# Order of the first loads and block norms, key products by feature tile, output slabs ahead of x, and pooled means in place

## The chip, the cores and the metric

The kernel runs on one core of a Trainium2 chip. The metric is the device time of the whole program in microseconds (us). The engines are TensorE (PE, with its weight loads listed apart as PEld), VectorE (DVE), ScalarE (ACT), GpSimd (POOL) and SyncE (SP), whose queue issues all DMA transfers of this kernel. Each engine runs its own instructions in the order that was fixed when the program was built. Semaphores make it wait for other engines.

## The reference

Two layers of a backbone run on 1024 latent tokens and 128 context tokens with 1024 features. Cut to what matters:

```python
shift1, scale1, gate1, shift2, scale2, gate2 = split(silu(cond) @ w_mod[l] + b_mod[l])
x = x + gate1 * mixer_l(rms_norm(x, g) * (1 + scale1) + shift1)
x = x + gate2 * conv_ffn(rms_norm(x, g2) * (1 + scale2) + shift2)
# layer 0: z = h @ w_in; queries, compressed keys/values and gated MLP from z; mixer = [attention | gMLP] @ w_out
c_kv = rms_norm(kv_c, g_kv)                   # 256 columns of z, beside 32 rotary ones
# layer 1: z = h @ w_in; mixer = [conv(a * sigmoid(gate)) | pool(p)] @ w_out
win = cs[:, hi, g] - cs[:, lo, g]             # window sums of 2, 4, 8, 16 tokens for four groups of 128 channels
pool = win / cnt - p                          # cnt is smaller at both ends of a sequence
pool = einsum("blgc,gcd->blgd", pool, w_pool) * s_pool
```

Outputs are both token sets after two layers, the normalised compressed keys/values and their rotary part for the context. Products are kept close to float32 by splitting each operand into a high and a low part and adding three products.

## The kernel before

**Tiling.** Features lie on the 128 partitions, in 8 feature tiles (`KT`). Tokens lie along the free side: 1154 columns, in three blocks `BLK` of 384, 384 and 386 (the last one holds 256 latent tokens, 2 empty columns and 128 context tokens). A normalised block is `hb[b]`, with a high and a low part for each feature tile. `mm3` (L74) issues the three products of one feature tile. `unit` (L54) loads a slab of weights into a `raw` buffer and splits it with ACT (L66) and DVE (L67) into a `wt` buffer; `weights(r, w)` says how many of each there are. PSUM has six banks `gp` for products and two `sm` for small ones.

**Order.** The program is written as one stream of calls. A planner with a model of the times gives each engine its fixed order: an instruction that is ready in the model goes first by its place in the stream, and `later(offset)` moves that place back. `fill` is a list of small steps, above all the modulation steps, which `drip` puts into the stream a few at a time with such an offset. `issue_after(ins)` keeps the instructions in its block behind `ins` on the same engine. `follow(a, b)` makes `a` wait for `b`.

**The start** (`even`, L463). Block 0 of x is loaded whole (L478). `mod_pe` (L118) loads eight slabs of w_mod for one chunk of the modulation (L124) and multiplies them on PE (L126). It runs for the scale (chunk 1) and then for the shift (chunk 0). `norm_blk` (L295) norms a block: ACT squares each feature tile (L257), the squares are added (`sq_sums`, L243: on DVE at L261 in the blocks of `FASTB`, else in pairs on POOL and DVE, L270 to L273), PE sums over partitions (L281), POOL takes the root (L589), PE spreads it (L290), DVE scales each feature tile in x itself (L318), and ACT and DVE write the shifted high and low parts into `hb` (L87, L88). For blocks 1 and 2, all eight tiles are scaled, then all eight are shifted. Their loads are kept behind the last slab of w_mod. Then `even_kv` (L624) loads three parts of evB and the first unit of evA. For three groups of three token tiles it multiplies the key/value columns, one token tile after the other (L658 to L660), and the first feature tile of queries (`q_proj`, L764). Chunks 2, 4 and 3 of layer 0's modulation are computed by DVE (`mod_dve_steps`, L140): 48 loads of 256 KB (L148), each followed by two multiply-adds into `macc` (L154, L157). They are in `fill` from this point on.

**The even output projection.** After the attention, `even` loads the three blocks of x again (L535), into the buffer that held the attention's values V. `out_half` (L552) loads four slabs of the output weights and runs eight output tiles of four feature tiles for each block (`out_tile`, L344). Each result is added to x by DVE (`residual`, L376, L383), which frees the PSUM bank. With three `raw` buffers, the first three slabs are loaded before the attention.

**The odd mixer** (`odd`, L1041). Twelve units of the input projection go by in the order conv 0, conv 1, pool 0, pool 1, conv 2, pool 2, pool 3, conv 3. A conv takes gates (ACT sigmoid into `sg`, L1087) and values (DVE product into `cv`, L1101). 8 of its 31 taps run on PE (`conv_pe`) and 23 on DVE (`conv_steps`, L1200), dripped from `fill`. A pool's projection is copied by ACT into a padded tile `xp` (L1124), which has the same tag `sg` and one buffer. `pool_windows` (L1204) adds shifted copies in two alternating buffers (L1220), writes mean minus input into the unpadded tile `pd` (L1226) and mends the ends of each sequence (L1229, L1230). `pool_out` (L1232) then splits `pd`, multiplies by w_pool (products named pp) and scales.

## Time and profile before

| | |
|---|---|
| median of 3 runs | 2791.72 us (2788.92 to 2794.14) |
| the profiled execution | 2793.62 us, of which the span of instructions is 2791.4 us |
| mean granted PE clock | 0.983 |
| PE busy | 2704.9 us, 97% of the span |
| DVE, ACT, POOL busy | 1839.2, 998.7, 394.6 us |
| DMA | 192.63 MB, 69 GB/s in the mean, one queue on SP |

In the rows below, L12 is line 12 of the kernel. "out<-in" names the tiles written and read. "x8" is a count. A bracket or the last column gives the idle time of the engine ahead of an instruction and what ended it. The granted clock is the share of full speed that the throttle leaves PE.

### The profile page before, as it was taken

The numbers are of one execution on the slowest core, as the hardware profiler recorded it, in microseconds if no ns is written. First come the engines' busy times: TensorE is split into PE (matmuls) and PEld (weight loads), VectorE is DVE, ScalarE is ACT, GpSimd is POOL, SyncE is SP. The second block draws the span as 40 slices with busy tenths as digits, with TensorE's granted clock in tenths as the row PEclk, the third lists the DMA queues.
The fourth block names the chain that finished last, engine by engine and source line by source line (L and its number), as shares of the span: only waits on it lengthen the run. The fifth ranks groups of instructions, "written<-read, shape, count | busy, mean of one in ns | idle before, by whom it ended". The sixth has DMA issues, their size and how long they took to land.

```text
span 2791.4 us, 38552 instructions
## 1 busy us (share of the span) xinstructions
PE 2704.9 (97%) x15636; PEld 2632.4 (94%) x15636; DVE 1839.2 (66%) x2864; ACT 998.7 (36%) x1671; POOL 394.6 (14%) x497
## 2 busy tenths in 40 slices
PE   7999999999999999999999999989999999999999
PEld 3897989999999999999999999889999999999999
DVE  5873777787786778855553878987555455554445
ACT  3543278782443222222223331324422222222331
POOL 2354165640200000000000200002000000000000
PEclk9999989999999999999999999999999999999999
DMA  7254210006143444311111011010011111111111
GB/s 277 71 151 110 86 37 24 25 11 226 55 125 117 132 129 130 120 46 46 38 46 38 10 46 39 27 53 28 26 40 44 41 43 41 44 38 39 46 46 68
DMA packets 92848, 192.63 MB, mean 69 GB/s; under 512 B 9472, under 2 KB 43136, under 8 KB 92672
## 3 DMA queue, kind: packets, MB, share of 16 engines
q1 hardware_dynamic: 92672, 190.18, 21.6%
q8 instruction: 123, 2.02, 0.3%
q14 instruction: 53, 0.43, 0.1%
HBM read 170.20 MB, written 19.95 MB: 68 GB/s over the span
## 4 chain that ended last, share of the span: by engine, by line
PE 85%; DVE 8%; ACT 2%; DMA 2%; POOL 1%; issue 1%; SPq 0%; DVEq 0%; ACTq 0%; POOLq 0%
PE fps L76 13%; PE fps L77 13%; PE fps L78 13%; PE ops L76 9%; PE ops L77 9%; PE ops L78 9%; PE av L989 2%; PE ptp L978 2%; PE ips L76 1%; PE ips L77 1%; PE ips L78 1%; PE Sa L1002 1%; DVE macc L157 1%; PE Sa L1004 1%; PE Sa L1003 1%
## 5 line engine op out<-in xcount | busy, mean ns | idle before, releaser
L77 PE MATMUL fps<-h,wt 128*128 128x384 f32 (+1 forms) x2112 | 713.2, 338 | 0.0
L76 PE MATMUL fps<-h,wt 128*128 128x384 f32 (+1 forms) x2112 | 711.2, 339 | 1.8 <-ACT h L87 0.9
L78 PE MATMUL fps<-h,wt 128*128 128x384 f32 (+1 forms) x2112 | 712.5, 338 | 0.0
L383 DVE SCALAR_TENSOR_TENSOR x<-ops,mod,x 128x384 f32<-128x384 f32 (+1 forms) x832 | 395.4, 512 | 233.7 <-PE ops L78 231.7
L67 DVE TENSOR_TENSOR wt<-raw,wt 128x1024 fp32r<-128x1024 f32 (+2 forms) x177 | 216.4, 1233 | 391.8 <-ACT wt L66 391.1
L77 PEld LDWEIGHTS fps<-h,wt 128*128 128x128 f32 x2112 | 398.6, 189 | 0.3
L76 PEld LDWEIGHTS fps<-h,wt 128*128 128x128 f32 x2112 | 396.2, 188 | 2.7 <-ACT h L87 1.2
L78 PEld LDWEIGHTS fps<-h,wt 128*128 128x128 f32 x2112 | 398.1, 189 | 0.1
L78 PE MATMUL ops<-act,wt 128*128 128x384 f32 (+1 forms) x1056 | 358.2, 339 | 0.0
L77 PE MATMUL ops<-act,wt 128*128 128x384 f32 (+1 forms) x1056 | 357.0, 338 | 0.0
L76 PE MATMUL ops<-act,wt 128*128 128x384 f32 (+1 forms) x1056 | 355.4, 339 | 0.0
L405 ACT ACTIVATE z<-fps 128x384 f32<-128x384 f32 (+1 forms) x264 | 128.9, 492 | 604.6 <-PE fps L78 604.2
L66 ACT ACTIVATE wt<-raw 128x1024 fp32r<-128x1024 f32 (+2 forms) x177 | 182.9, 1047 | 439.3 <-PE ops L78 322.6
L157 DVE SCALAR_TENSOR_TENSOR macc<-mraw,sc,macc 128x512 f32<-128x512 f32 x280 | 210.8, 783 | 41.5 <-DMA mraw<-in_wmod_dram 40.8
L76 PEld LDWEIGHTS ops<-act,wt 128*128 128x128 f32 x1056 | 199.6, 189 | 0.0
L78 PEld LDWEIGHTS ops<-act,wt 128*128 128x128 f32 x1056 | 198.6, 188 | 0.1
L77 PEld LDWEIGHTS ops<-act,wt 128*128 128x128 f32 x1056 | 198.7, 188 | 0.0
L1200 DVE SCALAR_TENSOR_TENSOR co<-cv,c_odw,co 128x1168 f32<-128x1168 f32 x92 | 132.8, 1446 | 21.0 <-ACT co L1193 20.2
L76 PE MATMUL ops<-h,wt 128*128 128x384 f32 (+1 forms) x384 | 133.1, 353 | 11.5 <-ACT wt L66 7.2
L414 DVE SCALAR_TENSOR_TENSOR c<-z,fdw,c 128x1153 f32<-128x1153 f32 x88 | 127.7, 1452 | 8.6 <-ACT c L412 7.7
L83 ACT ACTIVATE act<-c 128x1154 fp32r<-128x1154 f32 x44 | 51.5, 1172 | 226.7 <-DVE c L426 182.3
L77 PE MATMUL ops<-h,wt 128*128 128x384 f32 (+1 forms) x384 | 132.2, 344 | 0.4 <-DVE h L84 0.4
(281 smaller groups left out, 4550.7 us busy)
## 6 DMA issues: line engine op xcount, KB each, us to landing
raw<-in_fin_dram SPq DMA_DIRECT2D x88, 512.0 KB, 3.5
mraw<-in_wmod_dram SPq DMA_DIRECT2D x160, 256.0 KB, 2.8
raw<-in_fout_dram SPq DMA_DIRECT2D x44, 512.0 KB, 3.5
mraw<-in_wmod_dram SPq DMA_DIRECT2D x16, 512.0 KB, 9.0
fold<-macc SPq DMA_DIRECT2D x14, 512.0 KB, 3.0
macc<-fold SPq DMA_DIRECT2D x56, 128.0 KB, 3.1
x<-in_xt_dram SPq DMA_DIRECT2D x4, 1536.0 KB, 8.9
raw<-in_odin_dram SPq DMA_DIRECT2D x12, 512.0 KB, 3.5
```

The costliest lines, as they stand in the source:

```text
L66: nc.scalar.activation(wt[:, 0, :n], raw[:, :n], AF.Copy)
L67: nc.vector.tensor_tensor(out=wt[:, 1, :n], in0=raw[:, :n], in1=wt[:, 0, :n].bitcast(F32), op=ALU.subtract)
L76: mm(out, wh, ah, start=start, stop=False)
L77: mm(out, wh, al, start=False, stop=False)
L78: mm(out, wl, ah, start=False, stop=stop)
L157: nc.vector.scalar_tensor_tensor(out=a[:, c, :], in0=raw, scalar=self.sc[:, k, c:c + 1], in1=a[:, c, :], op0=ALU.mult, op1=ALU.add)
L383: nc.vector.scalar_tensor_tensor(out=xs, in0=ps[:, o:o + w], scalar=self.mod[l][:, gch * 8 + m, c:c + 1], in1=xs, op0=ALU.mult, op1=ALU.add)
L405: nc.scalar.activation(z[:, c0:c0 + n], ps[:, :n], AF.Copy)
L414: nc.vector.scalar_tensor_tensor(out=c[:, 1:T], in0=z[:, 0:T - 1], scalar=w[:, l, ti, 0:1], in1=c[:, 1:T], op0=ALU.mult, op1=ALU.add)
L978: nc.tensor.transpose(tp[:, a * P:(a + 1) * P], probs[j][:, kt * P:(kt + 1) * P], self.ident)
L989: nc.tensor.matmul(av[:, :256].rearrange("p (j t) -> p j t", j=2), V[:, kt, h, :], rhs, start=(kt == 0 and part == 0), stop=(kt == 8 and p ...
L1200: nc.vector.scalar_tensor_tensor(out=o, in0=cv[:, j:j + COW], scalar=dw[:, j:j + 1], in1=o, op0=ALU.mult, op1=ALU.add)
```

## The change

It has four parts.

1. **Start.** The first loads run in one fixed order on SP (`load_in_turn`): four slabs of chunk 1, block 0 of x, four slabs of chunk 1, eight slabs of chunk 0 with two parts of evB between them, block 1, the third part of evB, block 2, the first unit of evA. Block 0's squares are added on DVE. In blocks 1 and 2, scale and shift alternate by feature tile: the scale of tile k goes behind the shift of tile k - 2. The first loads of the early modulation wait for block 2's last shift (`gate`). Tiles `hb` get the width of their block.
2. **Key products.** The three token tiles of a group are multiplied together, feature tile by feature tile, in three PSUM banks.
3. **Even output.** The four slabs of the first half are traced ahead of the loads of x, which are kept behind the fourth slab's load.
4. **Pooled means.** The projection is copied straight into `pd`, which is now padded. Window sums run in place in one buffer, the ends are mended in the sums with a table that holds w/count instead of 1/count, and mean minus input is written over the input in `pd`. `pool_out` reads the padded tile, its last block in two pieces.

```diff
-        nc.sync.dma_start(out=raw[:, :n], in_=src)
+        self.loaded = (self.load_in_turn if turn else nc.sync.dma_start)(raw[:, :n], src)
...
+    def load_in_turn(self, dst, src):
+        if self.turn:
+            with self.tc.issue_after(self.turn.ins):
+                self.turn = self.nc.sync.dma_start(out=dst, in_=src)
+        else:
+            self.turn = self.nc.sync.dma_start(out=dst, in_=src)
+        return self.turn
+
+    def mod_pe(self, l, ch, pool, tag, rpool, between={}):
...
         for k in range(KT):
+            between.get(k, lambda: None)()
             raw = rpool.tile([P, 1024], F32, tag="mraw", name=self.nm("mraw"))
-            last = nc.sync.dma_start(out=raw, in_=self.ap["wmod"][l, k * P:(k + 1) * P, ch * D:(ch + 1) * D])
+            self.load_in_turn(raw, self.ap["wmod"][l, k * P:(k + 1) * P, ch * D:(ch + 1) * D])
...
+            ld = nc.sync.dma_start(out=raw, in_=self.ap["wmod"][l, k * P:(k + 1) * P, c0:c0 + 512])
+            if self.gate:
+                self.follow(ld, self.gate, "the first norm goes before")
+                self.gate = None if k else self.gate
...
-                load_x(0)
+                self.turn = None
+                wB = []
+                def load_w(i):
+                    s, n = ((0, 3), (3, 3), (6, 2))[i]
+                    wB.append(self.unit(ap["evB"][:, s * 288:(s + n) * 288], n * 288, turn=True))
+                self.mod_pe(0, 1, npool, "mrow", rpool, {4: lambda: load_x(0)})
                 add, chain, scaled, shifted = norm(0)
                 for k in range(KT):
                     add(k)
-                self.mod_pe(0, 1, npool, "mrow", rpool)
                 chain()
                 self.mod_scale(0, 0)
                 scaled()
-                last = self.mod_pe(0, 0, npool, "mrow", rpool)
+                self.mod_pe(0, 0, npool, "mrow", rpool, {4: lambda: load_w(0), 6: lambda: load_w(1)})
+                load_x(1)
+                load_w(2)
+                load_x(2)
+                wA = self.unit(ap["evA"][0], turn=True)
                 shifted()
-                with tc.issue_after(last.ins):
-                    load_x(1)
-                    load_x(2)
                 for b in (1, 2):
...
-                    scaled()
-                    shifted()
+                    los = []
+                    for k in range(KT):
+                        if k < 2:
+                            scaled([k])
+                        else:
+                            with tc.issue_after(los[k - 2].ins):
+                                scaled([k])
+                        los.append(shifted([k]))
+                    self.gate = los[-1]
...
         self.weights(3, 4)
+        ws = [self.unit(ap["evout"][1][u]) for u in range(4)]
         x = self.xpool.tile([P, KT, T], F32, tag="x", name="x1")
-        for b, (c0, n) in enumerate(BLK):
-            nc.sync.dma_start(out=x[:, :, c0:c0 + n], in_=ap["xt"][:, :, c0:c0 + n])
+        with tc.issue_after(self.loaded.ins):
+            for b, (c0, n) in enumerate(BLK):
+                nc.sync.dma_start(out=x[:, :, c0:c0 + n], in_=ap["xt"][:, :, c0:c0 + n])
...
-            for j in range(3):
-                ps = self.gp.tile([P, 512], F32, tag="gp", name=self.nm("kvps"))
-                o = ps[:, :288]
-                for k in range(KT):
+            pss = [self.gp.tile([P, 512], F32, tag="gp", name=self.nm("kvps")) for _ in range(3)]
+            for k in range(KT):
+                for j in range(3):
+                    o = pss[j][:, :288]
...
+            for j in range(3):
+                o = pss[j][:, :288]
                 nc.scalar.activation(kv[:, j, :], o, AF.Copy)
...
-                pd = pdt.tile([P, 4, T], F32, name="pd")
-                nc.gpsimd.memset(pd[:, :, LAT:CX], 0.0)
+                pd = pdt.tile([P, 4, PDW], F32, name="pd")
+                nc.gpsimd.memset(pd[:, :, 0:8], 0.0)
+                nc.gpsimd.memset(pd[:, :, 8 + LAT:PDX], 0.0)
+                nc.gpsimd.memset(pd[:, :, PDX + CTX:PDW], 0.0)
...
-                        xp = w1.tile([P, 1184], F32, tag="sg", name=self.nm("xp"))
...
-                                nc.scalar.activation(xp[:, d:d + n], ps[:, s:s + n], AF.Copy)
+                                nc.scalar.activation(pd[:, g, d:d + n], ps[:, s:s + n], AF.Copy)
...
-        self.pool_windows(g, xp, icnt, pd, pdt)
+        self.pool_windows(g, pd[:, g, :], icnt, pdt)
...
-        pp = w1.tile([P, 2, CVW], F32, tag="cs", bufs=1, name=self.nm("win"))
+        cur, s, L = xp, 1, PDW
+        win = pool.tile([P, 2, CVW], F32, tag="cs", bufs=1, name=self.nm("win"))[:, 0, :]
         while s < w:
             L -= s
-            nx = pp[:, i % 2, :]
-            i += 1
-            nc.vector.tensor_tensor(out=nx[:, :L], in0=cur[:, :L], in1=cur[:, s:s + L], op=ALU.add)
-            cur, s = nx, s * 2
+            nc.vector.tensor_tensor(out=win[:, :L], in0=cur[:, :L], in1=cur[:, s:s + L], op=ALU.add)
+            cur, s = win, s * 2
+        for (b0, n) in ((8, LAT), (PDX, CTX)):
+            wn = win[:, b0 - hw:b0 - hw + n]
             for e, c, m in ((0, 0, hw), (n - hw + 1, 8, hw - 1)):
                 if m:
-                    nc.vector.tensor_tensor(out=out[:, e:e + m], in0=wn[:, e:e + m], in1=icnt[:, g, c:c + m], op=ALU.mult)
-                    nc.vector.tensor_tensor(out=out[:, e:e + m], in0=out[:, e:e + m], in1=xp[:, b0 + e:b0 + e + m], op=ALU.subtract)
+                    nc.vector.tensor_tensor(out=wn[:, e:e + m], in0=wn[:, e:e + m], in1=icnt[:, g, c:c + m], op=ALU.mult)
+            xs = xp[:, b0:b0 + n]
+            nc.vector.scalar_tensor_tensor(out=xs, in0=wn, scalar=1.0 / w, in1=xs, op0=ALU.mult, op1=ALU.subtract)
...
+        if b == 2:
+            nc.gpsimd.memset(free[:, :, :, 256:258].bitcast(F32), 0.0)
...
-            self.split(ph[:, 0, :n], ph[:, 1, :n], pd[:, g, c0:c0 + n])
+            for (o, d, m) in [(0, 8 + c0, 384)] if b < 2 else [(0, 8 + c0, 256), (258, PDX, 128)]:
+                self.split(ph[:, 0, o:o + m], ph[:, 1, o:o + m], pd[:, g, d:d + m])
...
-FASTB = (1, 2)
+FASTB = (0, 1, 2)
```

More of the change, by code (lines that the diff above doesn't have):

```diff
@@ L51, in nm, with unit @@
         return f"{s}_{self.n}"
[L54 removed]
+    def unit(self, src, n=1024, gain=None, pool=None, turn=False):
         nc = self.nc
         raw = self.wraw.tile([P, 1024], F32, tag="raw", name=self.nm("raw"))
[L58 removed]
+        self.loaded = (self.load_in_turn if turn else nc.sync.dma_start)(raw[:, :n], src)
         wt = (pool or self.wsp).tile([P, 2, 1024], F32R, tag="wt", name=self.nm("wt"))
@@ L87, in split @@
             nc.scalar.activation(hi, src, AF.Identity, bias=shift)
-            nc.vector.scalar_tensor_tensor(out=lo, in0=src, scalar=shift, in1=hi.bitcast(F32),
-                                           op0=ALU.add, op1=ALU.subtract)
+            return nc.vector.scalar_tensor_tensor(out=lo, in0=src, scalar=shift, in1=hi.bitcast(F32),
+                                                  op0=ALU.add, op1=ALU.subtract)
     def consts(self, pool):
@@ L137, in mod_pe @@
             in1=self.bmod[:, l, ch * 8:(ch + 1) * 8].unsqueeze(2).to_broadcast([P, 8, 2]), op=ALU.add)
-        return last
     def mod_dve_steps(self, l, ch, pool, folded):
@@ L147, in step @@
             c0 = ch * D + h * 512
-            nc.sync.dma_start(out=raw, in_=self.ap["wmod"][l, k * P:(k + 1) * P, c0:c0 + 512])
+            ld = nc.sync.dma_start(out=raw, in_=self.ap["wmod"][l, k * P:(k + 1) * P, c0:c0 + 512])
+            if self.gate:
+                self.follow(ld, self.gate, "the first norm goes before")
+                self.gate = None if k else self.gate
             if k == 0:
@@ L322, in shift @@
             so = 0 if w == 0 else 24
-            self.split(hb[:, 0, k, o:o + m], hb[:, 1, k, o:o + m], src, self.mod[l][:, so + k, c:c + 1])
+            return self.split(hb[:, 0, k, o:o + m], hb[:, 1, k, o:o + m], src, self.mod[l][:, so + k, c:c + 1])
         def rest():
@@ L330, in rest, with scaled, shifted @@
                     shift(t, k, o, m, c)
-        def scaled():
-            for k in range(KT):
+        def scaled(ks=range(KT)):
+            for k in ks:
                 for (o, m, ro, c) in segs:
                     scale(x[:, k, c0 + o:c0 + o + m], k, o, m, ro, c)
-        def shifted():
-            for k in range(KT):
+        def shifted(ks=range(KT)):
+            for k in ks:
                 for (o, m, ro, c) in segs:
-                    shift(x[:, k, c0 + o:c0 + o + m], k, o, m, c)
+                    ins = shift(x[:, k, c0 + o:c0 + o + m], k, o, m, c)
+            return ins
         return (lambda k: add(x[:, k, c0:c0 + n]), chain) + ((scaled, shifted) if inplace else (rest,))
@@ L642, in even_kv @@
         nc.vector.memset(cst[:, 1:2], float(QD ** -0.5))
-        wB = [self.unit(ap["evB"][:, s * 288:(s + n) * 288], n * 288) for s, n in ((0, 3), (3, 3), (6, 2))]
-        wA = self.unit(ap["evA"][0])
         qc0 = c1.tile([P, 2, T], F32R, name="qc0")
@@ L1294, in new_hb @@
     def new_hb(self):
-        return [self.hpool.tile([P, 2, KT, BW], F32R, tag=f"h{b}", name=self.nm(f"h{b}")) for b in range(3)]
+        return [self.hpool.tile([P, 2, KT, BLK[b][1]], F32R, tag=f"h{b}", name=self.nm(f"h{b}")) for b in range(3)]
     def run(self):
         nc, tc, ap = self.nc, self.tc, self.ap
-        self.open, self.fill = {}, []
+        self.open, self.fill, self.gate = {}, [], None
         with ExitStack() as es:
```

31 lines of the change are left out of this document (10 added, 21 removed).

## The prediction

> **What bounds the kernel now.** I read the page first (the span and the busy time of TensorE), then the list of what TensorE waited for, then the busy time by stretch, and last the timelines of single engines around the longest waits.
>
> ```profile
> span 2791.4 us, 38552 instructions
> ...
> PE 2704.9 (97%) x15636; PEld 2632.4 (94%) x15636; DVE 1839.2 (66%) x2864; ACT 998.7 (36%) x1671; POOL 394.6 (14%) x497
> ```
>
> TensorE (PE) is busy for all but 86.5 us of the span, and the change removes no matrix product. So it can only win idle time of PE and the slow clock that follows idle time. The waits of PE, as line, releaser, total, count and longest, say where the idle time is:
>
> ```profile
> PE Sa L1002 <- ACT P L953: 12.4, 18, 1.8
> PE mps L126 <- DMA mraw<-in_wmod_dram: 11.5, 1, 11.5
> PE rb L290 <- DVE dg L288: 8.0, 2, 5.5
> PE ops L76 <- ACT wt L66: 7.2, 2, 6.1
> PE pp L76 <- ACT sg L1087: 5.4, 1, 5.4
> ```
>
> The first is the softmax inside attention, which the change doesn't touch. The other four are the start, the norms of blocks 1 and 2, the fourth slab of the even output projection, and a PSUM bank in the odd mixer. Each has a part of the change aimed at it. By stretch (start and end, length, then busy time and count of PE, PEld, DVE, ACT, POOL, then the granted clock, the DMA share and GB/s):
>
> ```profile
> 44.00:62.00 18.00, 16.47 (x108) 16.30 (x108) 17.37 (x34) 9.83 (x23) 5.31 (x5) 0.91 0.52 172
> 62.00:82.00 20.00, 12.72 (x54) 11.49 (x54) 15.48 (x34) 7.30 (x14) 4.41 (x6) 0.66 0.09 27
> 82.00:105.00 23.00, 23.00 (x159) 22.73 (x158) 20.39 (x55) 13.25 (x35) 10.02 (x13) 1.00 0.09 27
> 165.00:220.00 55.00, 49.84 (x299) 47.97 (x298) 42.66 (x81) 27.12 (x49) 41.11 (x41) 0.97 0.53 148
> 220.00:300.00 80.00, 79.21 (x413) 68.22 (x412) 28.58 (x42) 24.34 (x35) 21.85 (x17) 0.98 0.34 91
> 643.00:647.00 4.00, 3.96 (x12) 3.96 (x13) 2.11 (x3) 0.00 (x0) 0.00 (x0) 0.50 0.62 212
> 1789.00:1800.00 11.00, 5.05 (x17) 4.22 (x15) 11.00 (x24) 5.28 (x10) 0.00 (x0) 0.72 0.31 96
> ```
>
> Between 44 and 82 us VectorE (DVE) is nearly full, PE does 162 products where the next 23 us hold 159, and the granted clock falls to 0.66. So the front is bound by the norms on DVE.
>
> **A, the first loads and the block norms.** The rows needed are the DMA rate from 0 to 48 us in 40 slices, PE's first and last modulation products, the first key product, the first row of query products, and the last one:
>
> ```profile
> GB/s 0 23 77 181 273 388 393 420 389 362 335 427 416 413 423 421 388 394 382 408 413 406 410 410 416 386 407 401 416 395 384 380 379 379 372 380 377 407 386 356
> ...
> 11.51 19.29 PE L126 MATMUL mps<-mraw,sc 128*2 128x512 f32 x40 [11.51 <-DMA mraw<-in_wmod_dram]
> ...
> 38.24 5.31 PE L126 MATMUL mps<-mraw,sc 128*2 128x512 f32 x12
> ...
> 46.34 0.61 PE L658 MATMUL kvps<-wt,h 128*128 128x288 f32 x1 [0.92 <-ACT h L87]
> ...
> 85.48 0.29 PE L659 MATMUL kvps<-wt,h 128*128 128x288 f32 x1
> ...
> 87.33 0.34 PE L78 MATMUL qps<-h,wt 128*128 128x384 f32 x1
> ...
> 90.48 0.34 PE L78 MATMUL qps<-h,wt 128*128 128x384 f32 x1
> ...
> 104.72 0.34 PE L78 MATMUL qps<-h,wt 128*128 128x386 f32 x1
> ```
>
> Step 1. Block 0 of x (1536 KB, 1.57 MB) now goes ahead of every slab of w_mod, and PE waits for the first slab. At the 0.40 MB per us that the slices show, the block takes 3.9 us. With four slabs ahead of it, PE starts at 11.5 - 3.9 = 7.6 us. The fifth slab then lands after four slabs (1.3 us each) and the block, 9.1 us later, at 16.7. PE has used the first four by 7.6 + 16 x 0.44 (5.31 / 12) + 1.6 for the slow clock of the first products (19.29 less 40 x 0.44) = 16.3, so almost nothing is lost again. The modulation ends 3.9 us earlier, and the first key product, 2.8 us behind its end, moves from 46.3 to 42.4.
>
> Step 2. From there to the last query product (104.9 us before) PE has 216 key products and 72 query products. From 85.48 to 87.33 there are 14 key products, 0.132 us each. From 87.33 to 90.48 there are 18 query products, 0.175 us each. Together 28.5 + 12.6 = 41.1 us. I add 1.6 us for the slow clock behind the hand-over (9% of the first 18-us stretch), 2.5 us for the small products of two norms, and 3.4 us for stalls that I can't place: 42.4 + 48.6 = 91.0. That is 13.9 us earlier than now.
>
> This holds if the norms keep up. What they cost, from DVE's timeline, its groups from 0 to 95 us, and ScalarE's first square of block 1:
>
> ```profile
> 41.37 0.52 ACT L257 ACTIVATE nsum<-x 128x384 f32<-128x384 f32 x1 [4.35 <-DMA x<-in_xt_dram]
> ```
> ```profile
> 65.02 0.14 DVE L283 TENSOR_SCALAR ms<-st 128x3 f32<-128x3 f32 x1
> ...
> 69.57 4.29 DVE L318 SCALAR_TENSOR_TENSOR x<-x,scl,rb 128x384 f32<-128x384 f32 x8 [0.67 <-PE rb L290]
> ...
> 73.85 4.31 DVE L88 SCALAR_TENSOR_TENSOR h<-x,mod,h 128x384 fp32r<-128x384 f32 x8
> ```
> ```profile
> L157 DVE SCALAR_TENSOR_TENSOR macc<-mraw,sc,macc 128x512 f32<-128x512 f32 x14 | 11.8, 867 | 0.0
> L261 DVE TENSOR_TENSOR nsum<-nsum,nsq 128x384 f32<-128x384 f32 (+1 forms) x14 | 7.9, 568 | 0.4
> ```
>
> Block 1 lands at 41.4 now. Ahead of it three 256-KB loads of the early modulation, the first evA unit and the last evB part drop out or move behind (1.6 MB, 4 us), so it lands at 37.4. Its sums take 8 x 0.57 = 4.5 us, the chain to the scale 69.57 - 65.02 = 4.5 us, scale and shift 4.29 + 4.31 = 8.6 us: done by 56 with a microsecond lost to block 0. PE wants it at 42.4 + 15.6 (a third of the products, with the slow clock) = 58. Now the same block ends at 78.2, because sums, modulation steps and the other block share DVE. Alternating scale and shift per feature tile lets the key products, now by feature tile, start after one tile (9 x 0.132 = 1.2 us of PE per tile against 1.1 us of DVE). Block 0's sums on DVE instead of GpSimd (POOL) are 7 adds of 0.57 us, hidden under modulation products up to about 24 us; uncovered they would cost 4 us. I take **A = -14**. Its ends: -17 (no stall), -3 (only step 1, when PE's fixed order waits for a norm that is late).
>
> A rule that would take off 1.6 us more: the Trainium skill, "TensorE: Matmul & The Clock Gate", Part 1, has the clock halved after an idle window of about 3.4 us, so the 2.8-us hand-over would cost nothing. The row of 44 to 62 us with 0.91 behind just such a hand-over disagrees, and I stay with the row.
>
> **E, the modulation steps behind the gate.** The loads of the early modulation now wait for block 2's last shift. Eight loads with 16 DVE steps (14 in the row above, and two first multiplies) move from before 95 us to behind about 80. The first gated load stands in SP's in-order queue, with the loads of evK, evV and the constants behind it; those are wanted only by the key expansion near 91 us. The steps then meet this, in the groups from 105 to 220 us and in the list of POOL's power operations from 85 to 225 us (shortest, median, longest in ns):
>
> ```profile
> L157 DVE SCALAR_TENSOR_TENSOR macc<-mraw,sc,macc 128x512 f32<-128x512 f32 x42 | 32.2, 792 | 7.1 <-DMA mraw<-in_wmod_dram 7.1
> ```
> ```profile
> L589 POOL TENSOR_TENSOR qsc<-qms,mhalf x8: 1635/1646/2196, 186.2 to 222.4; 128x8 f32<-128x8 f32 x8
> ```
>
> POOL is busy 41 of the 55 us from 165 to 220, and its power operation stretches from 1.64 to 2.20 us beside DVE steps. If every one of the 16 steps stretches the POOL chain by 0.56 us, E is +8.8. If all go into the 51 us in which DVE is idle from 220 to 300, E is 0. I take **E = +2**, nearer the idle stretch.
>
> **B, the fourth slab ahead of x.** SP's queue, DVE, ScalarE and PE, and the landing times of slabs from 300 to 700 us:
>
> ```profile
> 624.21 3.74 SPq L535 DMA_DIRECT2D x<-in_xt_dram  x3
> 627.99 4.65 SPq L58 DMA_DIRECT2D raw<-in_evout_dram  x3
> ```
> ```profile
> 632.86 0.62 DVE L383 SCALAR_TENSOR_TENSOR x<-ops,mod,x 128x384 f32<-128x384 f32 x1
> ```
> ```profile
> 641.93 1.06 ACT L66 ACTIVATE wt<-raw 128x1024 fp32r<-128x1024 f32 x1 [10.21 <-DMA raw<-in_evout_dram]
> ```
> ```profile
> 643.04 0.69 PE L76 MATMUL ops<-h,wt 128*128 128x384 f32 x1 [6.06 <-ACT wt L66]
> ```
> ```profile
> DMA to landing us min/median/max: 3.3/5.2/13.9
> ```
>
> The fourth slab is issued behind three blocks of x and lands at 641.9, five us after PE has finished six tiles with the first three. Issued first, it needs 3.3 us and lands near 627.5. That saves 6.1 us and the half clock of the 4 us behind it (2 us). x then lands 1.3 us later. The first residual is at 632.9, and the sixth bank fills only at 637 (643.04 - 6.06), so it stays covered; without that cover it would cost its 1.3 us. **B = -7.5**, ends -4 (the split waits in ScalarE's order behind those of the attention) and -8.
>
> **C, pooled means in place.** ScalarE and PE in the odd mixer:
>
> ```profile
> 1768.58 1.32 ACT L1124 ACTIVATE xp<-ips 128x384 f32<-128x384 f32 x4 [3.01 <-DVE pd L1230]
> ...
> 1794.75 1.24 ACT L1087 ACTIVATE sg<-ips 128x384 f32<-128x384 f32 x3
> ```
> ```profile
> 1795.27 0.69 PE L76 MATMUL pp<-h,wt 128*128 128x384 f32 x1 [5.43 <-ACT sg L1087]
> ```
>
> xp and sg share one buffer. So the last gates can't leave PSUM until the fourth window sum is done, and PE runs out of banks. With the means in the padded tile, sg waits only for the product of conv 2, long done. This saves 5.4 us and about 1.7 us of slow clock behind it (the stretch from 1789 to 1800 us is granted 0.72, and this first product takes 0.69 us, twice the 0.34 of a query product). The fourth group's split is then late next: its sums start some 4 us earlier, at the end of its projection, and end near 1790, just when PE wants them; I leave 1 us for that. Halved edge steps and 9 POOL memsets fewer, against four more small splits on both engines, are hidden: PE has bank slack there (some 1 us on DVE if not). **C = -6**, ends 0 and -8. The smaller h tiles and the scaled edge table add no instruction and cost nothing.
>
> **Sum.** -14 + 2 - 7.5 - 6 = -25.5. The profiled execution took 2793.6 us, its span and 2.2 us around it, which gives 2768.1. It lies 1.9 us over the median of the runs, 2791.7; from there it is 2766.2. I put down 2767.
>
> **Rivals.**
> R1, DVE and POOL take the front's gain back: the norms of blocks 1 and 2 hold PE once more, so A is -9, and the deferred steps all meet the POOL chain, so E is +8.8. Then -13.7, 2780. For it: DVE is at 20.4 of 23 and 42.7 of 55 us in those stretches. Against: 51 us of idle DVE follow.
> By the Trainium skill, "SBUF — State Buffer", on the port pair that DVE and GpSimd share, the loser blocks for a whole instruction; with 0.79 us a step E would be 12.7 and the time 4 us more. The 0.56 us of the row agrees in kind.
> R2, the pooled part doesn't do what it says: the fourth window sum on DVE ends as late as now, and PE waits for its split instead. C is 0, 2774. For it: DVE is busy for all of the 11 us from 1789 to 1800. Against: that work started late because of the shared buffer.
> R3, slower: the eight deferred loads run on into attention, where DVE must also give PE its row maxima and takes its queue in order. From the chain of waits:
>
> ```profile
> 296.51 2.83 DMA mraw<-in_wmod_dram
> ```
>
> Each load then blocks DVE for 2.8 us of landing and two steps of 0.79: 4.4 us. Eight make 35; with E's +2 out, that is -27.5 + 35 = +7.5, 2801. It decides from seven loads on. Against it: the idle 51 us before attention.
> R4, no stall anywhere: all best ends, -33, 2760.6.
>
> **How the numbers follow.** Forecast 0.52, R1 0.20, R2 0.12, R3 0.08, R4 0.08. No change means within 0.2% (5.6 us), about what a measurement of this kernel can tell. The forecast's own range is 2760 to 2777. For 8 in 10 I go from 2754 to 2790: R4 and a little more below, R1 and a lost B above. Faster 0.85; within 0.2% 0.07 (R1 with a lost B); slower 0.08 (R3).
>
> **What would show it.** A: the first modulation product near 7.6 us, the last query product of the first feature tile of queries near 91, and a granted clock over 0.9 from 44 to 82. E: 16 macc steps later and POOL's power operations no longer than 2.2 us. B: no wait for wt in the first output half, its fourth slab issued ahead of x. C: no pp wait for sg. Wrong would be a new wait of over 5 us on st or rb, or key products that wait for h.

## The result and the profile after

The median of five runs is 2761.25 us (2758.74 to 2766.95), against 2792.59 us for five runs of the kernel before on the same chip. The ratio is 0.9892, with a 95% interval of 0.9878 to 0.9906: faster by 1.1%. The forecast was 2767 us, the range 2754 to 2790. The profiled execution took 2759.46 us, with a span of 2757.3.

The waits of PE in the changed kernel, in the columns of the list shown of before (line, releaser, total, count, longest):

```profile
PE Sa L1033 <- ACT P L984: 12.2, 17, 2.0
PE mps L138 <- DMA mraw<-in_wmod_dram: 7.3, 2, 7.0
PE ops L78 <- ACT h L85: 4.6, 2, 2.5
PE st L295 <- DVE nsum L287: 4.3, 2, 2.5
PE ips L79 <- DVE h L90: 4.1, 8, 1.0
PE pp L80 <- DVE wt L69: 3.6, 1, 3.6
...
PE kvu L745 <- ACT ckvT L734: 2.5, 5, 0.9
PE rb L304 <- DVE dg L302: 2.3, 1, 2.3
```

All four waits that the change was aimed at are gone or shorter: the start 11.5 to 7.0, rb 8.0 to 2.3, the slab's 6.1 and the wait of pp for sg (5.4) to nothing. Of rb's 8.0, only 5.5 lay in the front, and these are gone; 2.5 belonged to a norm in the odd mixer, where the 2.3 remain. But the wait for wt ahead of pp is new, and those for nsum (0.9 before) and ckvT (1.2 before) have grown.

The front by stretch in the changed kernel (busy time and count of PE, PEld, DVE, ACT and POOL, granted clock, DMA share, GB/s), and PE's timeline at the first modulation product, the first key product and the last query product of the first tile:

```profile
44.00:62.00 18.00, 16.51 (x105) 15.77 (x106) 17.16 (x37) 11.69 (x27) 7.27 (x10) 0.93 0.19 62
62.00:82.00 20.00, 20.00 (x142) 19.70 (x143) 19.90 (x51) 13.45 (x34) 3.12 (x3) 1.00 0.01 2
```
```profile
6.95 5.28 PE L138 MATMUL mps<-mraw,sc 128*2 128x512 f32 x6 [6.95 <-DMA mraw<-in_wmod_dram]
...
42.37 0.40 PE L687 MATMUL kvps<-wt,h 128*128 128x288 f32 x1 [0.91 <-ACT h L89]
...
90.33 0.34 PE L80 MATMUL qps<-h,wt 128*128 128x386 f32 x1
```

From 62 to 82 us PE is full at full clock, where it was 12.7 us busy at 0.66.

To see where the other time went, the span is cut into the same stages in both traces, by the first product of each. The rows show attention, the even output, the first FFN, the odd mixer in three parts, and the second FFN, with boundaries rounded to 1 us, before and then after:

```profile
346.00:624.00 278.00, 260.08 (x1921) 248.83 (x1920) 214.25 (x459) 220.78 (x531) 162.37 (x263) 0.94 0.08 22
624.00:736.00 112.00, 105.94 (x592) 105.06 (x591) 85.79 (x153) 34.41 (x60) 18.64 (x17) 0.97 0.50 161
736.00:1585.00 849.00, 847.88 (x4834) 846.48 (x4832) 572.91 (x831) 252.57 (x328) 47.13 (x36) 1.00 0.27 83
1585.00:1790.00 205.00, 197.53 (x1090) 192.80 (x1090) 172.90 (x209) 61.18 (x106) 18.78 (x35) 0.99 0.10 33
1790.00:1820.00 30.00, 23.50 (x110) 22.13 (x111) 25.97 (x42) 12.54 (x24) 3.07 (x3) 0.83 0.12 36
1820.00:1947.00 127.00, 114.80 (x618) 110.86 (x617) 103.75 (x166) 44.72 (x86) 20.94 (x20) 0.93 0.12 38
1947.00:2786.00 839.00, 838.09 (x4759) 837.50 (x4758) 438.88 (x596) 240.87 (x305) 3.53 (x3) 1.00 0.13 43
```
```profile
336.00:608.00 272.00, 253.87 (x1926) 241.27 (x1924) 213.07 (x458) 219.60 (x531) 162.47 (x263) 0.98 0.08 23
608.00:717.00 109.00, 105.45 (x592) 103.71 (x591) 86.28 (x155) 34.70 (x60) 18.16 (x17) 0.98 0.50 165
717.00:1561.00 844.00, 842.58 (x4832) 841.33 (x4830) 571.73 (x830) 252.34 (x328) 47.97 (x36) 1.00 0.27 84
1561.00:1765.00 204.00, 196.73 (x1090) 191.13 (x1090) 172.86 (x203) 63.84 (x115) 16.76 (x26) 0.99 0.10 33
1765.00:1792.00 27.00, 22.25 (x107) 20.69 (x108) 25.22 (x35) 9.64 (x18) 2.83 (x2) 0.87 0.13 40
1792.00:1917.00 125.00, 114.23 (x617) 111.02 (x616) 103.20 (x169) 45.47 (x87) 20.31 (x21) 0.93 0.12 39
1917.00:2752.00 835.00, 834.09 (x4764) 833.48 (x4762) 439.67 (x595) 241.02 (x305) 4.24 (x3) 1.00 0.13 43
```

With the unrounded starts, the 34.1 us between the two spans split as follows. The key expansion is counted from the end of the last query product of the first tile to the end of the last product kvu.

| stage | after less before (us) | what it is |
|---|---|---|
| to the last query product of the first tile | -14.4 | part 1 and 2 |
| key expansion | +6.4 | in part the deferred modulation steps |
| queries and gated MLP, to the first score | -1.5 | |
| attention | -6.8 | same work, idle time 18.1 and 17.9, clock 0.98 against 0.94 |
| even output | -3.05 | part 3 |
| odd mixer, three parts | -5.2 | part 4 |
| two FFNs | -9.7 (4.84 each) | PE idle 0.9 to 1.4 us in each, in either kernel |

The FFN row is the surprise: nothing of the change seems to touch the FFNs, and they pay more than a quarter of the gain.

### The profile page after: what moved, and what is told of

Same layout as the page of the kernel before. It is cut to its first block, busy times and chain, and to the rows that moved or that the text cites. A ratio compares the mean times of both kernels' runs of the same rounds, so it can differ in the third digit from the quotient of the medians.

```text
span 2757.3 us, 38543 instructions
## 1 busy us (share of the span) xinstructions
PE 2682.7 (97%) x15636; PEld 2605.0 (94%) x15636; DVE 1835.9 (67%) x2858; ACT 998.8 (36%) x1675; POOL 389.2 (14%) x484
## 4 chain that ended last, share of the span: by engine, by line
PE 83%; DVE 8%; DMA 3%; ACT 3%; POOL 2%; issue 1%; SPq 0%; DVEq 0%; POOLq 0%; ACTq 0%
PE fps L78 13%; PE fps L79 13%; PE fps L80 13%; PE ops L78 8%; PE ops L79 8%; PE ops L80 8%; PE av L1020 2%; DMA mraw<-in_wmod_dram 2%; PE ptp L1009 2%; PE ips L79 1%; PE ips L78 1%; PE ips L80 1%; DVE macc L171 1%; PE Sa L1033 1%; PE Sa L1034 1%
## 6 DMA issues: line engine op xcount, KB each, us to landing
x<-in_xt_dram SPq DMA_DIRECT2D x4, 1536.0 KB, 11.7
```

## The experiments

**Where the FFNs' gain comes from.** `width_only` is the kernel before with one word of the diff:

```diff
-        return [self.hpool.tile([P, 2, KT, BW], F32R, tag=f"h{b}", ...) for b in range(3)]
+        return [self.hpool.tile([P, 2, KT, BLK[b][1]], F32R, tag=f"h{b}", ...) for b in range(3)]
```

> The kernel before with one edit: the three h tiles get 384, 384 and 386 columns in place of 386 each. Nothing else changes, and no work is left out. Width theory: in the trace of the changed kernel a product of 384 columns that reads h takes 173.3 ns from start to start in the mean, against 175.8 before, while those that read the act tiles take 175.3 to 175.9 in both. On about 5,900 such products that is 14.6 us, of which 2 x 4.8 lie in the two FFNs. So 2778 us, with each FFN 4.8 us shorter. Rival, the recorded prediction: the narrower tiles cost and gain nothing, 2792; then the FFNs of the changed kernel were shorter for another reason, such as a better granted clock in that one profile.

Measured: 2783.0 us, ratio 0.9967 (0.9958 to 0.9977), so -9.2 us (-6.4 to -11.7). The FFNs are 4.0 and 4.8 us shorter, and products of 384 columns that read h start 173.3 ns apart, as in the changed kernel, against 175.8 before (means over some 2,100 neighbouring pairs in each FFN). The width alone makes nearly all of the FFNs' gain. That part of the theory holds; the rest of the 14.6 us was not seen, and in this profile attention was 2.3 us longer than before, at a clock of 0.94.

The group rows of the second FFN by shape, for the first of three products per tile, show it on one line each: before, then `width_only` (busy time, mean ns; each product overlaps the next, so one lasts longer than the distance between two starts):

```profile
L76 PE MATMUL fps<-h,wt 128*128 128x384 f32 x704 | 238.0, 339 | 0.0
```
```profile
L76 PE MATMUL fps<-h,wt 128*128 128x384 f32 x704 | 236.0, 336 | 0.0
```

**Which property of the tile it is.** `one_block_narrow` gives the three blocks different widths, in the kernel before:

```diff
-... tile([P, 2, KT, BW], F32R, tag=f"h{b}" ...
+... tile([P, 2, KT, (386, 384, 392)[b]], F32R, tag=f"h{b}" ...
```

> The kernel before with h tiles of 386, 384 and 392 columns, so that rows of one feature tile lie 1544, 1536 and 1568 bytes apart in blocks 0, 1 and 2. No work is left out; the products read 384, 384 and 386 columns as ever. Row-distance theory: a product's time hangs on where its row begins. Block 0 stays at 175 to 178 ns from start to start, with a pattern over the eight feature tiles, block 1 goes to 173.3 and even, so the second FFN is 2.4 us shorter by block 1 alone (837.2 us from 839.7). For block 2, if rows 32 bytes apart in their beginnings are enough, its 386-column products go from 177.1 to 174.2 ns and the FFN to 834.2; if only longer steps are enough, they stay at 177. Rival, that the total size or place of the tiles in memory does it and not the row: blocks 0 and 1 come out alike.

Measured: 2790.2 us in one run. The second FFN took 841.1 us. Block 1, with even rows, did not become fast: its products lie 176.6 ns apart, in every feature tile alike. Block 0 keeps its pattern over the feature tiles (170 to 182 ns), and block 2 with rows of 1568 bytes stays at 176.7. So the row distance doesn't decide by itself. What differs for block 1 from `width_only` is the place: the tile ahead of it is 128 bytes longer per partition, so all of its rows begin 128 bytes further on. The weights lie at the same addresses in both programs, so it isn't the other operand.

`act_wide` tries the same on the other operand, in the changed kernel:

```diff
-                a = cp.tile([P, 2, T], F32R, tag="act", name=self.nm("act"))
-                self.split(a[:, 0, :], a[:, 1, :], u)
+                a = cp.tile([P, 2, 1184], F32R, tag="act", name=self.nm("act"))
+                self.split(a[:, 0, :T], a[:, 1, :T], u)
```

> The changed kernel with one edit: the act tiles of the FFNs get 1184 columns in place of 1154, of which 1154 are used, so that the low halves begin 4736 bytes behind the high ones and not 4616. No work is left out. Row-distance theory: the FFN's output products read act at 175 to 178 ns where h at even rows takes 173.3; with even rows the 384-column ones go to 173.3, about 2.4 ns on 2,112 products, some 5 us, both FFNs 2 to 3 us shorter (second one 832.4 from 834.8), 2756. Rival: the act products are slow for another reason (what the other engines write beside them, or the residual reads behind them) and nothing changes, 2761.

Measured: ratio 0.9906 (0.9890 to 0.9923), 2763.46 us: no gain in the whole. In its profile the even output, which the edit leaves as it is, took 4.2 us longer than in the changed kernel, with waits of 4.4 us for nsum and 1.5 for x. By stage, the first FFN is 2.5 us shorter (841.8) with act products 173.4 ns apart, and the second 0.4 us longer (835.3) with 175.6. Half of the expectation came true. The program's allocation says what differs: in the first FFN the wide tiles begin at multiples of 128 bytes, in the second 64 bytes off. `wide_moved` is `act_wide` with the second FFN's pools shifted by 64 bytes:

```diff
+            if l:
+                nc.gpsimd.memset(pool.tile([P, 16], F32, name="shift"), 0.0)
```

> The changed kernel with the act tiles 1184 columns wide and, in the second FFN only, one unused tile of 64 bytes per partition allocated ahead of its pools, which moves z, c and act of that FFN by 64 bytes. No work is left out. Place theory, as the last runs left it: it is not the row distance but where in memory an operand begins. In the first FFN the wide act tiles begin at multiples of 128 bytes and their 384-column products took 173.4 ns; in the second they begin 64 bytes beside such a multiple and stayed at 175.6, the second FFN at 835.3 us. Moved by 64 bytes, the second FFN's act products go to 173.4 too and its length to 832.8 (1,056 products x 2.3 ns). The first FFN stays at 841.8. In all -5 us against the changed kernel, 2756. Rival: the two FFNs differ for another reason, the place changes nothing, 835.3 and 175.6 stay; the whole is then 2 to 3 us under the changed kernel at best, 2759 to 2763.

Measured: the second FFN takes 832.77 us and its act products are 173.41 ns apart. The place theory had said 832.8 and 173.4. The rows of the second FFN's output products by shape, in `act_wide` and then in `wide_moved`:

```profile
L80 PE MATMUL ops<-act,wt 128*128 128x384 f32 x352 | 119.0, 338 | 0.0
```
```profile
L80 PE MATMUL ops<-act,wt 128*128 128x384 f32 x352 | 118.3, 336 | 0.0
```

The first FFN took 842.9. The whole is 2758.8 us, ratio 0.9876 (0.9859 to 0.9892). This is the lowest median of all, but its interval overlaps that of the changed kernel; only the FFNs' 3.5 us are shown.

**What the gate does.** `no_gate` takes one line out of the changed kernel:

```diff
-                    self.gate = los[-1]
```

> The changed kernel without the gate: the first loads of the early modulation no longer wait for the last shift of block 2. No work is left out. Theory, that the gate moved the cost: in the changed kernel the key expansion (last query product of the first tile to last key or value product) is 6.3 us longer than before, with 28 modulation steps on VectorE in it. Without the gate half of them come early again; the key expansion should be 3 to 6 us shorter, while the norms of blocks 1 and 2, which share VectorE with the steps, end later and the last query product of the first tile moves from 90.7 to 94 to 100. In all 0 to +4 us, 2761 to 2765. Rival, that the gate is what makes the front faster: the last query product moves back to some 100 to 105, +9 to +14, 2771 or more. Second rival, that the steps hide beside the norms: -6, 2755.

Measured: 2773.92 us, ratio 0.9937 (0.9920 to 0.9953), 0.45% or 12.6 us more than with the gate. The key expansion is 4.1 us shorter (46.0 against 50.1), as expected, but the last query product of the first tile falls back from 90.7 to 100.5. The first rival holds. The stretches of the front and of the key expansion without the gate, then the key expansion with it, and last PE's two longest waits of the front without it:

```profile
62.00:82.00 20.00, 16.00 (x84) 14.94 (x85) 18.62 (x44) 11.12 (x22) 3.19 (x3) 0.69 0.06 19
82.00:101.00 19.00, 18.90 (x130) 18.62 (x128) 16.35 (x43) 11.83 (x29) 8.49 (x13) 1.00 0.19 57
101.00:147.00 46.00, 42.24 (x225) 34.80 (x226) 36.40 (x68) 25.48 (x44) 22.26 (x19) 1.00 0.42 113
```
```profile
91.00:141.00 50.00, 44.15 (x223) 34.76 (x222) 43.94 (x83) 25.30 (x45) 25.95 (x22) 0.97 0.50 140
```
```profile
PE st L295 <- DVE nsum L275: 4.8, 1, 4.8
PE rb L304 <- DVE dg L302: 2.7, 1, 2.7
```

With 16 modulation steps on DVE in the front, where the gate leaves 4, PE waits for the norm's sums and the clock is down to 0.69, near the 0.66 of the kernel before. The rest of parts 1 and 2 keeps 4.6 us; the load order, the alternating norms and the sums on DVE were not tried apart. The key expansion has 16 steps here, as in the kernel before, and still takes 2.4 us more than the 43.7 there.

**What the key products by feature tile do.** `by_token_tile` undoes part 2:

```diff
-            for k in range(KT):
-                for j in range(3):
+            for j in range(3):
+                for k in range(KT):
```

> The changed kernel with one part undone: the key products of a block run by token tile again, each over all eight feature tiles, not by feature tile. No work is left out. Recorded prediction's mechanism: by feature tile TensorE keeps pace with the norm, 1.2 us of products for each feature tile against 1.1 us on VectorE. By token tile the first third ends only with the last feature tile, near 50.5 us, and 48 products of 0.132 us stand behind it, so the first block ends near 57 in place of 52.4: +4.7 for the first block, and as much again for each later block whose norm TensorE has caught up with; 2766 to 2775. Rival: the delay in the first block only uses up time in which the later norms end anyway, so that the last query product of the first tile stays at 90.7 within 1.5 us: 2761 to 2763.

Measured: the last query product of the first tile at 92.14, 1.5 us later, so by the trace the rival holds, at the edge of its bound, and part 2 is worth 1.5 us of the front. The whole is 2765.91 us, ratio 0.9908 (0.9892 to 0.9924), which alone would fit the theory's lower end. But the profiled run is 8.1 us longer than the changed kernel's, and 6.6 of that is attention, which this edit doesn't touch.

**The deferred steps.** `drip_one` sets KVDRIP from 2 to 1 in the changed kernel.

```diff
-KVDRIP = 2
+KVDRIP = 1
```

> The changed kernel with one number changed: the key expansion lets one modulation step through at each place in the order instead of two, so that half of the 28 steps of that stretch move to the stretch behind it, where VectorE is idle for some 50 us. No work is left out. Theory, that these steps crowd VectorE and stretch GpSimd's power operations there: the key expansion becomes 3 us shorter (half of the 6.3 us by which the changed kernel's is longer than before), the rest stays, so -3, 2758. Rival, that the key expansion is longer for another reason (its own chain, now started earlier, meets later transfers): no change, 2761, or +2 if the steps that moved meet the next stage.

Measured: 2787.9 us, ratio 0.9987 (0.9978 to 0.9997), 26.5 us slower than the changed kernel. The key expansion did get shorter, by 5.0 us up to the first product of the query expansion (71.9 from 76.9). But 12 steps ran on into attention, which became 34 us longer. PE's longest waits from 330 to 400 us:

```profile
PE mps L191 <- DVE macc L171: 20.0, 2, 15.5
```

PE's own order has the sums of the last modulation behind the first twelve scores and ahead of the others, so it stands while the steps come in, most of them behind the landing of a load. This is the mechanism of the prediction's slower rival, R3, in its place. That the 34 us are near its price of 35 is chance: R3 counted eight loads at 4.4 us, and here six loads (12 steps) hold PE for 20.0 us, 4.5 of them while the last step took 5.25 us, for which the trace shows no reason. In all PE is idle for 24 us more than in the changed kernel's attention, and the other 10 us lie in products at a lower clock (0.76 from 330 to 400 us). The other parts' gains still keep this kernel under the one before. `drip_kv1_q2` also lets two steps through in the query expansion (QDRIP from 1 to 2), so that as many are done by then as in the changed kernel.

```diff
-KVDRIP = 2
+KVDRIP = 1
...
-QDRIP = 1
+QDRIP = 2
```

> The changed kernel with two numbers changed: the key expansion lets one modulation step through at each place instead of two, the query expansion two instead of one, so that 34 of 54 entries are through by the end of the queries, as against 35 in the changed kernel (25 in the run with one step each). No work is left out. Theory, that the 34 us lost in that run came from steps that ran on into attention: attention is back at 271 to 280 us with no 15-us wait for macc, and the key expansion stays at 72, not 77. What the query expansion takes (41.9 us) decides the rest: as it was, 2756; with 0.56 us for each of ten more steps beside GpSimd's power operations, 47.5 and 2762. Rival: the 5 us of the key expansion don't come from the steps themselves but are lost wherever these stand, 2761 or more, with the query expansion 5 us longer or attention late again.

Measured: 2763.14 us, ratio 0.9902 (0.9887 to 0.9917). Attention is back at 277.5 us with no wait for macc at its start. The key expansion is 4.5 us shorter by the same bounds (72.3), the query expansion 3.5 us longer (45.4). Most of what the one gains the other loses.

**Where the slab's gain went.** `slab_only` is the kernel before with part 3 alone.

```diff
+        ws = [self.unit(ap["evout"][1][u]) for u in range(4)]
         x = self.xpool.tile([P, KT, T], F32, tag="x", name="x1")
-        for b, (c0, n) in enumerate(BLK):
-            nc.sync.dma_start(...)
+        with tc.issue_after(self.loaded.ins):
+            for b, (c0, n) in enumerate(BLK):
+                nc.sync.dma_start(...)
```

> The kernel before with one part alone: the four slabs of the second half of the even output projection are issued ahead of x, which waits for their issue. No work is left out. Recorded prediction: the 6.06-us wait for the fourth slab goes, and the half clock behind it, -7.5 us (-4 to -8), so 2784. Rival from the trace of the changed kernel: the wait comes back in another place. There TensorE waits 2.5 us for the sums of the norm at 683 us, because GpSimd's order has the adds of the deferred modulation ahead of the sums, and 1.1 us in two smaller waits; the output stage was 3.1 us shorter in all, of which 1 us belongs to the narrower h tiles. So -2 us, 2790, which is within what can be told from no change, and the trace decides: a wait for nsum of over 2 us in the second output half.

Measured: ratio 0.9992 (0.9983 to 1.0002), so -2.2 us (-4.7 to +0.6); the even output is 3.5 us shorter in the trace. The rival holds. PE's longest wait from 620 to 730 us in `slab_only`, and POOL's timeline around that wait in the changed kernel:

```profile
PE st L281 <- DVE nsum L273: 2.6, 1, 2.6
```
```profile
675.39 1.01 POOL L286 TENSOR_TENSOR nsq<-nsq,nsq 128x384 f32<-128x384 f32 x1 [1.11 <-ACT nsq L271]
679.48 1.29 POOL L181 TENSOR_TENSOR macc<-macc 128x512 f32<-128x512 f32 x1 [3.08 <-DMA macc<-fold]
680.85 0.74 POOL L182 TENSOR_TENSOR macc<-macc 128x256 f32<-128x256 f32 x1
681.54 1.01 POOL L286 TENSOR_TENSOR nsq<-nsq,nsq 128x384 f32<-128x384 f32 x1
```

POOL stands 3.1 us for a DMA, because the fold of the later modulation is ahead of the norm's sums in its order. The products that came earlier meet this. How much they lose varies: in the nine profiles with part 3 and the sums on POOL, PE waits 2.4 to 6.3 us for nsum in this stage, which takes 108.9 to 113.5 us; in the four without part 3 it waits 6.0 to 6.4 us for wt, and the stage takes 111.4 to 112.5. `sums_on_dve` moves those sums:

```diff
-... fast=inplace and b in FASTB)
+... fast=(inplace and b in FASTB) or (l == 0 and w == 1))
```

> The changed kernel with one helper's work moved: the pair sums of the squares in the norm behind the even output projection go to VectorE, not GpSimd. No work is left out. Theory, that the slab's part gave back 2.5 us because GpSimd has the adds of the deferred modulation ahead of those sums: the wait for nsum (2.5 us, at 683) goes and the time is -2.5 to -3, 2758. Rival: VectorE, which also makes the residuals and splits of that stretch, now ends as late, and the wait comes back for x or for h: 0 to +4, 2761 to 2765.

Measured: 2760.31 us, ratio 0.9887 (0.9872 to 0.9903), no change from the changed kernel that can be told. The even output is 4.5 us shorter (104.8), and the first FFN 5.4 us longer (849.7), with waits of 1.7 us for macc, 0.9 and 0.4 for h at its start and a clock of 0.97 in its first 50 us. The rival comes nearest, but the wait moved on by a whole stage, which neither expectation had.

**Where the pooled means' gain went.** `pooled_and_width` is `width_only` with part 4.

```diff
-                xp = w1.tile([P, 1184], F32, tag="sg", name=self.nm("xp"))
...
-                nc.scalar.activation(xp[:, d:d + n], ps[:, s:s + n], AF.Copy)
+                nc.scalar.activation(pd[:, g, d:d + n], ps[:, s:s + n], AF.Copy)
...
-        self.pool_windows(g, xp, icnt, pd, pdt)
+        self.pool_windows(g, pd[:, g, :], icnt, pdt)
```

> The kernel before with two parts: the pooled means in place in the padded tile, and the narrower h tiles, without which the padded tile finds no room. To be read against the run with the narrower tiles alone. No work is left out. Recorded prediction: -6 us beside that run, since no product waits for sg any more. Rival from the trace of the changed kernel: -2.5 us beside that run, because the wait for sg (5.4 us) is followed by a wait for wt (3.6 us) and one of 0.7: the slab of the pooled projection is loaded last of four into four buffers and gets its own only when the last projection into the mixer ends, so its split ends as late as the products that want it. The trace decides: a pp wait for wt of 3 us or more.

Measured: 2775.72 us, ratio 0.9945 (0.9930 to 0.9960), against 0.9967 for the width alone: -6 us, with some 5 us of uncertainty. In the traces the odd mixer is 355.7 against 361.0 us, -5.2. So the term is nearer the prediction than the rival, though the wait for wt is there. PE's waits in this stage, before and then in the changed kernel, show why:

```profile
PE pp L76 <- ACT sg L1087: 5.4, 1, 5.4
PE ops L76 <- ACT h L83: 4.3, 2, 2.5
PE st L281 <- DVE early L261: 3.0, 1, 3.0
```
```profile
PE ops L78 <- ACT h L85: 4.6, 2, 2.5
PE pp L80 <- DVE wt L69: 3.6, 1, 3.6
PE st L295 <- DVE nsum L287: 1.8, 1, 1.8
```

The new wait of 3.6 us takes back most of the 5.4, and the wait for early (3.0) goes as well. `owp_first` loads the pooled projection's slab first of the four:

```diff
+                        wps = self.unit(ap["owp"], 4 * P)
                         units.extend(self.unit(ap["odout"][1][u]) for u in range(3))
-                        units.append(self.unit(ap["owp"], 4 * P))
+                        units.append(wps)
```

> The changed kernel with one load moved: the slab of the pooled projection is loaded ahead of the three output slabs of the odd mixer, not behind them. No work is left out. Theory, that the part with the pooled means gave back 3.5 us because this slab gets its buffer last: the pp wait for wt (3.6 us) and the smaller one (0.7) go, and -3.5 to -4.3, 2757. Rival: the third output slab is now the late one, wanted 3 us after the pooled products, and the wait moves to it: 0 to -1, 2761.

Measured: 2763.75 us, ratio 0.9898 (0.9881 to 0.9916): no gain. The wait for wt is gone, and the longest from 1770 to 1925 us are now these, with the one for cs grown from 0.9 us before:

```profile
PE cps L78 <- ACT cs L85: 6.5, 1, 6.5
PE ops L78 <- ACT h L85: 4.3, 2, 2.5
PE st L295 <- DVE early L275: 3.1, 1, 3.1
```

The rival held in its time, not in its mechanism: what is late is not the third slab but the work of ACT and DVE for the convolution. All waits of PE in this stretch add up to 18.3 us here, to 15.4 in the changed kernel and to 18.8 before. In the changed kernel DVE is busy for 25.2 of the 27 us from 1765 to 1792, and a PE that comes earlier waits further on.

## Why the prediction was right, and where it was not

The time was 6 us below the forecast of 2767, inside the range and inside the forecast's own range. Its steps did less well than its sum. By stage, the four terms came to -14.4 + 6.4 - 3.05 - 5.2 = -16.3 us, not -25.5. What brought the sum back, and past the forecast, is 9.7 us in the FFNs and 6.8 in attention, where the prediction had nothing. That the time came out so near was luck; that the front would gain 14 us was not.

**A, -14: right in size and place.** PE starts at 6.95 (forecast 7.6), the first key product stands at 42.37 (42.4), the last query product of the first tile ends at 90.66 (91.0), and the clock is 0.93 and 1.00. What carries most of it is the gate: without it 9.8 us of the 14.4 are lost. The prediction had put the freed DVE under A and the gate's cost under E, and the runs bear out both.

**E, +2: undersized, and for another reason.** The key expansion takes 6.4 us more. The step that failed is that POOL's power operation stretches beside DVE's steps and sets the price. From 80 to 230 us its shortest, median and longest in the changed kernel are:

```profile
L620 POOL TENSOR_TENSOR ksc<-kms,mhalf x10: 1636/1854/2581, 102.6 to 141.6; 128x8 f32<-128x8 f32 x10
```

The longest is over the bound of 2.2 us, yet nine of them took 17.3 us against 16.0 (rows below). So they explain 1.3 of the 6.4 us at most. (16 steps of 0.56 us would be 9.0, not the 8.8 of the prediction; nothing hangs on it.) By the Trainium skill, "SBUF — State Buffer", section "SBUF: two separate sides", on the port pair that DVE and GpSimd share, the one that comes second blocks for a whole instruction. The longer operations agree with that in kind. The groups of the key expansion, before (105 to 149 us) and after (91 to 141):

```profile
L589 POOL TENSOR_TENSOR ksc<-kms,mhalf 128x8 f32<-128x8 f32 x9 | 16.0, 1780 | 19.1 <-DVE kms L724 19.0
...
L157 DVE SCALAR_TENSOR_TENSOR macc<-mraw,sc,macc 128x512 f32<-128x512 f32 x14 | 9.9, 746 | 0.8 <-DMA mraw<-in_wmod_dram 0.8
```
```profile
L171 DVE SCALAR_TENSOR_TENSOR macc<-mraw,sc,macc 128x512 f32<-128x512 f32 x26 | 18.6, 743 | 1.2 <-DMA mraw<-in_wmod_dram 1.2
L620 POOL TENSOR_TENSOR ksc<-kms,mhalf 128x8 f32<-128x8 f32 x9 | 17.3, 1934 | 16.7 <-DVE kms L755 16.7
L745 PE MATMUL kvu<-wt,ckvT 128*128 128x512 f32 x39 | 16.8, 430 | 3.2 <-ACT ckvT L734 2.5 <-DVE V L760 0.7
```

Twelve more steps put 8.7 us on DVE's queue, and PE waits for what stands behind them: it is idle for 5.9 of the 50.1 us, against 2.2 of 43.7 before, and the other 2.8 us lie in products at a clock of 0.97, where it was 1.00. The gate accounts for 4.1 of the 6.4 us. The 2.4 us that are there without it, with as many steps as before, come from something else, which no run settles. That the steps would find the 51 idle microseconds after 220 us was wrong: they stay where the fixed order lets them through (from the end of this stage to the first score, 64 steps run in either kernel), and where they were let through later the time was lost again.

**B, -7.5: oversized.** The 6.06 us went, and no wait for wt is left in the first output half. The stage gained 3.05 us, none of it by the width that shows (112.3 us in `width_only`, 112.4 before); alone, part 3 is worth -2.2 by the times. "It stays covered" held for x: PE waits for nothing from the start of the stage to 663 us. The step that failed is that the sum ends there. The prediction looked at the residual and the bank behind the earlier products, but not at POOL, whose fixed order holds the norm's sums behind a transfer, at 2.5 us here and more in other profiles.

**C, -6: right within a microsecond, by another sum.** It measured -5.2 in the changed kernel and in `pooled_and_width`. The wait for sg went, the slab of the pooled projection came in its place (3.6 and 0.7 us, where I had left 1 us for the fourth split), and the wait for early, which the prediction did not count, went too.

**The h tiles, at nothing: wrong.** "The smaller h tiles ... add no instruction and cost nothing" was true of the instructions and false of the time: 9.2 us by the times of the run that has only them.

**What stays open.** Attention was 6.8 us shorter in the changed kernel's profile, with 18.1 us of idle time against 17.9 and a clock of 0.98 against 0.94. Seven profiles with the gate have it at 271.0 to 277.9 us, six without at 276.0 to 280.3. Two rows for kernels that leave attention as it is, `by_token_tile` with the gate and `no_gate` without:

```profile
336.00:614.00 278.00, 259.06 (x1922) 247.80 (x1921) 214.06 (x459) 221.52 (x531) 162.50 (x263) 0.95 0.08 22
```
```profile
343.00:619.00 276.00, 257.66 (x1921) 246.18 (x1920) 213.76 (x459) 220.67 (x531) 163.06 (x263) 0.96 0.08 22
```

The means differ by 3.8 us, and the ranges overlap. In all thirteen PE is idle for 17.6 to 19.3 us of the stage, and its length goes with the granted clock, from 271.0 us at 0.987 to 280.3 at 0.939. So the 6.8 us are a matter of the clock granted in these executions. Whether the change has a part in that clock was not settled.

Of the rivals, R1 came true in half (E at 6.4 of its 8.8, A not at all), and R2's idea, a wait in place of the one removed, appeared in B and in C, but not for the window sum that R2 named. R3 did not come: the last deferred step starts at 326.0 us, 10.5 us ahead of attention, as in the kernel before, and `drip_one` shows what lies on the other side of those 10.5 us.

## What to carry to other kernels

When a wait is removed, look down the order of every engine for what the earlier arrival meets next; here two of the four waits removed were partly replaced, the deferred steps crowded another stage, and of four attempts to mend these (`drip_one`, `drip_kv1_q2`, `sums_on_dve`, `owp_first`) each moved the loss once more. Deferring work off a full engine paid here because the stage that it leaves gained 9.8 us and the next lost 4.1, but it must be through before the next stage that takes its results in order. That a change of a tile's size adds no instruction doesn't make it free: compare the distance between equal products before and after.

## What was unexpected of the hardware

In this kernel the time of a matrix product depends on where in memory its moving operand begins. Same shape, no wait, full granted clock: 384 columns of four bytes lie 173.3 ns apart at one place, 176.6 with all rows begun 128 bytes further on, and between 170 and 182 ns, by feature tile, where rows are 1544 bytes apart. For act, a shift by 64 bytes took 175.6 to 173.4. At some 1.3% of the products' time this is larger than part 3 of this change. `wide_moved` shows it most cleanly, since the tile's size and the weights' place stay the same. The rule by which the place decides is not settled, and it was tried only for these places. It isn't the distance to a multiple of 128 bytes alone: the rows of h begin 32 bytes behind one both at 173.3 and at 176.6 ns.
